# Down weights of a mixture-of-experts layer fetched with four consecutive rows per partition

## The chip, the cores and the metric

The kernel runs on one core of one Trainium2 chip, alone. The metric is the device time of one execution in microseconds, the median of the runs. Times from the trace are in microseconds (us) from the start of the span, or in nanoseconds (ns) where marked.

## The reference, cut to what matters

Two layers, each a mixer followed by a hierarchical mixture of experts (MoE) with 16 SwiGLU experts. There are 256 tokens of width 1024, the hidden width of an expert is 512, and every token goes to two experts. All arrays are float32.

```python
for e in range(N_EXPERTS):                                # 16
    hid = jax.nn.silu(xt @ w_gate[e]) * (xt @ w_up[e])    # (tokens, 1024) @ (1024, 512)
    y = y + gates[:, e:e + 1] * (hid @ w_down[e])         # (tokens, 512) @ (512, 1024)
```

The weights of one layer's experts are 96 MiB: 2 MiB each of gate, up and down per expert.

## The kernel before

**Stream of weights.** The host code builds one list, `order`, of pieces of 1 MiB, in the order in which they are consumed: for an expert two pieces of gate and two of up in turn (`gu`), and two of down (`dn`). `pump` issues them from the SP queue into 15 rotating buffers named `raw` (two more where space allows), each 128 partitions by 2048 float32, so a piece can be issued only when the piece that held its buffer has been used up. All of these issues are line 252. Experts that are not fixed beforehand (all but the first two) are known only when the router of that layer has run.

**Layout of the pieces.** Gate and up go in as `(p k) n -> p k n` with four of eight `k`: partition p gets four consecutive rows of 512 values, one run of 8 KiB. Down goes in as `(j p) n -> p j n` with two of four `j`: partition p gets rows 128 j + p of 1024 values, two separate runs of 4 KiB.

**Tasks.** Each expert's tokens are gathered into slots; the slots are cut into 20 tasks of 64 or 32 (8 of 64, 12 of 32), in the order `SEQ`. For a task, `gate_up` keeps the tokens stationary (`win`, or `hs` for expert 0) and streams the weights (`raw`). Since 64 or 32 tokens fill a half or a quarter of the array's columns, G = 2 or 4 matmuls on different column groups run at the same time, each with its own slice of the 512 hidden columns: 256 columns each at G = 2, 128 at G = 4. I call such a set of G matmuls a round. Every float32 matmul leaves two records, so a half task (4 k, gate and up) is 16 rounds in either form: 32 records at G = 2, 64 at G = 4. `hidden` takes Silu and the product, `turn` transposes 128 hidden columns at a time into `ht`, and `down` multiplies `ht` with the down weights, reading `raw` with a step of 8 values (32 bytes) because the 1024 outputs are kept as n k with k = 8. `project` moves the result out, and `combine` adds it up per token.

**Order.** SP and TensorE run in the order that is written out: first half of gate and up of task i+1, transposes of task i, second half of task i+1, down of task i. After task 9 (`LEFT`) every engine loads a count and passes a branch (`whatever_is_left`, lines 1433 and 1434; its body, `further`, runs only if tokens did not fit and is not entered here).

Of the kernel before, what the change touches and what calls it, by code (L numbers as in the profile page):

```python
# [19 lines left out]
P = 128  # L20
# [6 lines left out]
DE = 512  # L27
# [85 lines left out]
def trunk_kernel(ctx: ExitStack, tc: tile.TileContext, a, out, dbg=None):  # L113
    nc = tc.nc
    V, A, G, T = nc.vector, nc.scalar, nc.gpsimd, nc.tensor
# [9 lines left out]
    def bank(i):  # L125
        return pp.tile([P, 512], F32, name=f"b{i}", tag=f"b{i}")
# [4 lines left out]
    def k3(ap, k=KD):  # L131
        return ap.rearrange("p (k n) -> p k n", k=k)

    def mm(o, l, r, start=False, stop=False):
        T.matmul(o, l, r, start=start, stop=stop, skip_group_check=True)  # L135
# [30 lines left out]
    def moe(l):  # L166
        def at(name, p):
            if p < FIXED:
                return a[name][l, p]
            return lambda v: a[name][l, v]  # L170

        def gu(p):
            for h in range(2):
                for name in ("moe_w_gate", "moe_w_up"):
                    def cut(w, h=h):
                        return w.rearrange("(p k) n -> p k n", k=KD)[:, 4 * h:4 * h + 4, :]
                    order.append(("w", (name, l, p), (at(name, p), cut), 4))

        def dn(p):
            for h in range(2):  # L180
                def cut(w, h=h):
                    return w.rearrange("(j p) n -> p j n", p=P)[:, 2 * h:2 * h + 2, :]
                order.append(("w", ("moe_w_down", l, p), (at("moe_w_down", p), cut), 2))

        gu(0)
        for i, t in enumerate(TASKS):
            u = TASKS[i + 1] if i + 1 < len(TASKS) else None
            early = t["first"] and t["p"] < FIXED
            if early:
                dn(t["p"])  # L190
            if u and u["first"]:
                gu(u["p"])
            if t["first"] and not early:
                dn(t["p"])
# [265 lines left out]
    for i in range(4):  # L460
        b = bank(i)
# [841 lines left out]
    def place(rr, e, base, G):  # L1303

        pe = sb.tile([P, 2, P], BF, name="pe", tag="pt")
        for t in range(2):
            V.tensor_scalar(pe[:, t, :].rearrange("p (g w) -> p g w", g=G),
                            iota[:, 0:P // G].unsqueeze(1).to_broadcast([P, G, P // G]),
                            rr[:, t, e:e + 1], float(-base), op0=OP.subtract, op1=OP.is_equal)
        return pe  # L1310

    def moe_layer(l, before, then):
# [25 lines left out]
        def load_window(o, base, n, tag=None):  # L1338
            w = sb.tile([P, KD, n], F32, name="win", tag=tag or "sq", bufs=1 if tag else 3)
            A.copy(w, hs[:, :, ds(o + base, n) if base else ds(o, n)])  # L1340
            return w

        def slots(e, base, pe):
            b = bankbf(7)
            g = b[:, 512:518].bitcast(F32)
            for t in range(2):
                mm(g, pe[:, t, :], g3[:, t, e, :], start=(t == 0), stop=(t == 1))
            for t in range(2):
                T.transpose(b[:, t * P:(t + 1) * P], pe[:, t, :], identb)
            gs = sb.tile([P, 1], F32, name="gs", tag="gs1")  # L1350
            V.tensor_reduce(gs, g, AX.X, OP.add)
            ptt = sb.tile([P, S], F32R, name="ptt", tag="rs")
            A.copy(ptt, b[:, 0:S])
            return ptt, gs


        def gate_up(w, wts, b, G, halves=(0, 1)):
            n, r = DE // G, P // G
            for h in [x for f in halves for x in (2 * f, 2 * f + 1)]:
                i, src = h % 2, k3(wts[h], 4)  # L1360
                for kk in range(4):
                    for g in range(G):
                        mm(b[g * r:(g + 1) * r, i * n:(i + 1) * n], w[:, h // 2 * 4 + kk, :],
                           src[:, kk, g * n:(g + 1) * n], start=(h + kk == 0), stop=(h + kk == 6))

        def hidden(b, gs, G, tag="hid"):
            n = DE // G
            hid = sb.tile([P, n], F32, name="hid", tag=tag)
            A.activation(hid, b[:, 0:n], AF.Silu)  # L1369
            V.scalar_tensor_tensor(hid, hid, gs, b[:, n:2 * n], op0=OP.mult, op1=OP.mult)  # L1370
            return hid

        def turn(hid, b, G, tag="ht"):
            n, m = DE // G, DE // G // P
            for c in range(m):
                T.transpose(b[:, c * P:(c + 1) * P], hid[:, c * P:(c + 1) * P], ident)  # L1376
            ht = sb.tile([P, m, G, P // G], F32, name="ht", tag=tag)
            A.copy(ht.rearrange("p c g s -> p (c g s)"), b[:, 0:n])  # L1378
            return ht

        def down(ht, wts, G, bs2=(6,)):

            n, r, m, q = D // G, P // G, DE // G // P, KD // G
            ys = [bank(i) for i in bs2]
            y = [ys[g % len(ys)] for g in range(G)]
            for j in range(4):
                src = k3(wts[j // 2], 2)[:, j % 2, :].rearrange("p (n k) -> p n k", k=KD)
                for g in range(G):
                    mm(y[g][g * r:(g + 1) * r, 0:n], ht[:, j % m, j // m, :], src[:, :, q * g:q * (g + 1)],
                       start=(j == 0), stop=(j == 3))  # L1390
            return y
# [5 lines left out]
        def further(p, base, bk):  # L1397

            def load(name, tag, cut):
                r = sb.tile([P, 2048], F32, name="raw", tag=tag)  # L1400
                e = p if p < FIXED else nc.sync.value_load(exi[0:1, p:p + 1], min_val=0, max_val=NE - 1)
                nc.sync.dma_start(k3(r, 4 if name != "moe_w_down" else 2), cut(a[name][l, e]))
                return r

            tags = ("f8", "m8", "f8", "m8")
            wts = []
            for h in range(2):
                for name in ("moe_w_gate", "moe_w_up"):
                    wts.append(load(name, tags[len(wts)],
                                    lambda w: w.rearrange("(p k) n -> p k n", k=KD)[:, 4 * h:4 * h + 4, :]))  # L1410
                if h == 0:
                    b = bank(bk)
                    pt, gs = slots(p, base, place(rr, p, base, 2))
                    o = nc.scalar.value_load(ofi[0:1, 16 + p:17 + p], min_val=0, max_val=2 * S - base)
                    w = load_window(o, base, 64, "m8b")
                gate_up(w, wts, b, 2, (h,))
            ht = turn(hidden(b, gs, 2, "r8"), b, 2, "m8b")
            wts = [load("moe_w_down", tags[h], lambda w: w.rearrange("(j p) n -> p j n", p=P)[:, 2 * h:2 * h + 2, :])
                   for h in range(2)]
            y = down(ht, wts, 2)[0]  # L1420
            y2 = sb.tile([P, 2, 512], F32R, name="y2", tag="r8")
            A.copy(y2[:, 0, :], y)
            V.tensor_sub(y2[:, 1, :], y, y2[:, 0, :].bitcast(F32))
            for n in range(2):
                yx = y2[:, n, :]
                for kk in range(4):
                    for g in range(2):
                        k, rows = 4 * g + kk, slice(64 * g, 64 * g + 64)
                        mm(acc[k // 2][:, (k % 2) * S:(k % 2 + 1) * S],
                           yx.rearrange("p (n k) -> p k n", k=4)[rows, kk, :], pt[rows, :])  # L1430
# [10 lines left out]
        start, banks, wins, gates, packs, hid, gu, dw_ = {}, {}, {}, {}, {0: pe}, {}, {}, {}  # L1441
        n = len(TASKS)
# [30 lines left out]
        def first_half(i):  # L1473
            t = TASKS[i]
            p = t["p"]
            if t["first"]:
                gu[p] = take_all([(x, l, p) for x in ("moe_w_gate", "moe_w_up") * 2])
            banks[i] = bank(4 + i % 2)
            gate_up(wins[i], [w for w, _ in gu[p]], banks[i], P // t["n"], (0,))
            if t["last"]:  # L1480
                for _, x in gu[p][0:2]:
                    free(x)
# [48 lines left out]
        for i, t in enumerate(TASKS):  # L1531
# [11 lines left out]
            j = 0  # L1543
            if i + 2 < n:
                prepare(i + 2)
                if TASKS[i + 2]["pack"] > TASKS[i + 1]["pack"]:
                    j = TASKS[i + 2]["pack"]
# [25 lines left out]
    h = rms(drain_ada)  # L1573
# [21 lines left out]
    with in_order():  # L1595
# [23 lines left out]
        for t in range(2):  # L1619
            for i in range(4):  # L1620
                c = slice(2 * i, 2 * i + 2)
                src = k3(bk[i][:, t * S:(t + 1) * S], 2)
# [32 lines left out]
```

## Time and profile before

| | us |
|---|---|
| Runs before | 803.02, 805.72, 806.88 (median 805.72) |
| Profiled execution, its time | 803.79 |
| Profiled execution, its span | 802.0 |
| DMA data read from HBM | 285.69 MB |
| MoE of layer 0: stream of its routed pieces | about 185 to 406 |
| MoE of layer 1: stream of its routed pieces | about 564 to 783 |

[...] "A <- B" in a list of waits means that engine A stood idle until B was done.

### The profile page before, as it was taken

What the parts mean: (1) busy time and instruction counts of PE and PEld (TensorE: products, weight loads), DVE (VectorE), ACT (ScalarE), POOL (GpSimd) and SP (SyncE); (2) the same over time, 40 slices, a digit from 0 to 9 for tenths busy, and PEclk for the clock granted to TensorE, in tenths of its full rate; (3) what the DMA queues carried; (4) which work ended last, traced back from release to release, by engine and by line L of the source; (5) the groups of instructions that cost most, each with busy time, mean ns of one, the idle gap of its engine ahead of it and who ended that gap; (6) DMA issues with size and microseconds to landing.
All of it is one profiled execution on the core that took longest, in us unless ns stands there. A gap on an engine that the chain in (4) does not pass through costs nothing. (4 is left out here: it accounts for less than half of the span.)

```text
span 802.0 us, 18126 instructions
## 1 busy us (share of the span) xinstructions
PE 695.3 (87%) x7589; PEld 478.9 (60%) x7589; DVE 375.4 (47%) x866; ACT 236.8 (30%) x530; POOL 13.2 (2%) x33
## 2 busy tenths in 40 slices
PE   4699899978999959997669989998999995999765
PEld 3376358956666637544338878775666664755433
DVE  2516788877322212211158999997722231221114
ACT  3211143041222213211055326473322221321114
POOL 0010002000000000000000000000000000000000
PEclk9799899999999979999899999999999998999988
DMA  8989999967999999999999999321899999999991
GB/s 300 370 290 402 400 406 409 418 253 300 350 416 412 417 407 407 416 418 415 415 400 397 398 409 409 103 81 54 335 401 415 408 419 392 411 416 413 417 406 66
DMA packets 70029, 288.12 MB, mean 359 GB/s; under 512 B 8909, under 2 KB 11273, under 8 KB 53544
## 3 DMA queue, kind: packets, MB, share of 16 engines
q1 hardware_dynamic: 69928, 286.77, 90.1%
q8 instruction: 63, 1.03, 0.5%
q14 instruction: 38, 0.31, 0.1%
HBM read 285.69 MB, written 1.06 MB: 358 GB/s over the span
## 5 line engine op out<-in xcount | busy, mean ns | idle before, releaser
L135 PE MATMUL b<-raw,win 128*32 128x128 f32 (+1 forms) x3712 | 198.5, 309 | 36.3 <-DVEq L1434 16.9
L135 PEld LDWEIGHTS b<-raw,win 128*32 128x32 f32 (+1 forms) x3712 | 141.2, 120 | 85.7 <-issue 28.9
L1512 DVE TENSOR_TENSOR yp<-b,yp 32x256 fp32r<-32x256 f32 (+1 forms) x128 | 62.5, 488 | 143.5 <-ACT yp L1511 143.3
L135 PE MATMUL b<-raw,ht 128*32 128x256 f32 (+1 forms) x1024 | 113.5, 460 | 15.1 <-DMA raw<-in_moe_w_down_dram 15.0
L1511 ACT CAST yp<-b 32x256 fp32r<-32x256 f32 (+1 forms) x128 | 53.3, 417 | 131.0 <-PE b L135 93.2
L135 PEld LDWEIGHTS b<-raw,ht 128*32 128x32 f32 (+1 forms) x1024 | 42.1, 119 | 69.8 <-issue 34.5
L319 DVE SCALAR_TENSOR_TENSOR raw<-raw,csil 128x1024 f32<-128x1024 f32 x56 | 74.6, 1332 | 4.3 <-DMA raw<-in_w_ada_dram 3.2
L1370 DVE SCALAR_TENSOR_TENSOR hid<-hid,gs,b 128x128 f32<-128x128 f32 (+1 forms) x40 | 16.0, 401 | 113.4 <-ACT hid L1369 113.4
L914 DVE SCALAR_TENSOR_TENSOR ac<-hqk,dw,ac 128x256 f32<-128x256 f32 x120 | 50.7, 481 | 0.3
L135 PE MATMUL b<-h,raw 128*128 128x256 f32 x192 | 44.8, 392 | 5.3 <-ACT h L584 2.9
L135 PE MATMUL b<-hh,whf 128*128 128x256 f32 x160 | 41.7, 299 | 4.1 <-DVE whf L588 3.7
L135 PEld LDWEIGHTS b<-h,raw 128*128 128x128 f32 x192 | 37.1, 196 | 13.1 <-ACT h L584 3.8
L1369 ACT ACTIVATE hid<-b 128x128 f32<-128x128 f32 (+1 forms) x40 | 12.8, 320 | 105.5 <-PE b L135 105.5
L135 PE MATMUL b<-mx,raw 128*128 128x256 f32 x160 | 40.6, 409 | 0.0
L135 PEld LDWEIGHTS b<-mx,raw 128*128 128x128 f32 x160 | 38.8, 335 | 1.0 <-issue 0.8
L135 PE MATMUL b<-hl,whf 128*128 128x256 f32 x128 | 37.2, 290 | 0.4 <-DVE hl L849 0.4
L1378 ACT COPY ht<-b 128x128 f32<-128x128 f32 (+1 forms) x40 | 12.3, 308 | 84.6 <-PE b L1376 84.5
L1471 DVE TENSOR_REDUCE gs<-b 128x1 f32<-128x3 f32 x40 | 6.4, 161 | 65.9 <-PE b L135 65.5
L135 PE MATMUL b<-ptt,yp 128*128 128x256 f32 x224 | 34.4, 295 | 2.4 <-ACT yp L1511 1.6
L135 PEld LDWEIGHTS b<-hh,whf 128*128 128x128 f32 x160 | 29.7, 200 | 7.5 <-DVE whf L588 4.1
L135 PEld LDWEIGHTS b<-ptt,yp 128*128 128x128 f32 x224 | 28.4, 188 | 9.3 <-ACT yp L1511 6.6
L135 PE MATMUL b<-raw,h 128*128 128x512 f32 x64 | 31.5, 640 | 0.0
(287 smaller groups left out, 825.9 us busy)
## 6 DMA issues: line engine op xcount, KB each, us to landing
raw<-in_moe_w_gate_dram SPq DMA_DIRECT2D x64, 1024.0 KB, 13.1
raw<-in_moe_w_up_dram SPq DMA_DIRECT2D x64, 1024.0 KB, 14.7
raw<-in_moe_w_down_dram SPq DMA_DIRECT2D x64, 1024.0 KB, 16.5
raw<-in_w_ada_dram SPq DMA_DIRECT2D x48, 1024.0 KB, 15.8
raw<-in_ev_w_in_dram SPq DMA_DIRECT2D x10, 1024.0 KB, 13.1
raw<-in_od_w_in_dram SPq DMA_DIRECT2D x10, 1024.0 KB, 18.4
raw<-in_ev_w_out_dram SPq DMA_DIRECT2D x4, 1024.0 KB, 15.0
raw<-in_od_w_out_dram SPq DMA_DIRECT2D x4, 1024.0 KB, 14.0
```

Of the source, the lines that this page charges most:

```text
L135: T.matmul(o, l, r, start=start, stop=stop, skip_group_check=True)
L319: ins = V.scalar_tensor_tensor(acc, src, csil[:, k:k + 1], acc, op0=OP.mult, op1=OP.add)
L914: V.scalar_tensor_tensor(ac[:, m, :], src, dw[:, m, j:j + 1], ac[:, m, :], op0=OP.mult, op1=OP.add)
L1369: A.activation(hid, b[:, 0:n], AF.Silu)
L1370: V.scalar_tensor_tensor(hid, hid, gs, b[:, n:2 * n], op0=OP.mult, op1=OP.mult)
L1378: A.copy(ht.rearrange("p c g s -> p (c g s)"), b[:, 0:n])
L1471: V.tensor_reduce(gates[i], g, AX.X, OP.add)
L1511: A.copy(yh[o[0], o[1], :], src)
L1512: V.tensor_sub(yl[o[0], o[1], :], src, yh[o[0], o[1], :].bitcast(F32))
```

## The change

Down pieces are cut as `(p j) n -> p j n` with j = 4: partition p now gets rows 4 p + 2 h and 4 p + 2 h + 1 of half h, which lie next to each other in memory, one run of 8 KiB. Down's contraction for a given j is then over the hidden features 4 p + j, so the hidden columns have to come out in that order: `gate_up` streams the columns j, 4 + j, 8 + j, ... in place of a block of neighbours. Its moving operand is thus read with a step of four values (16 bytes). The output columns in PSUM are still contiguous. The number of matmuls, weight loads, DMAs and bytes is the same; `down`, `turn` and everything after them are untouched.

```diff
         def dn(p):
             for h in range(2):
                 def cut(w, h=h):
-                    return w.rearrange("(j p) n -> p j n", p=P)[:, 2 * h:2 * h + 2, :]
+                    return w.rearrange("(p j) n -> p j n", j=4)[:, 2 * h:2 * h + 2, :]
                 order.append(("w", ("moe_w_down", l, p), (at("moe_w_down", p), cut), 2))
...
         def gate_up(w, wts, b, G, halves=(0, 1)):
-            n, r = DE // G, P // G
+
+            n, r, m = DE // G, P // G, 4 // G
             for h in [x for f in halves for x in (2 * f, 2 * f + 1)]:
                 i, src = h % 2, k3(wts[h], 4)
                 for kk in range(4):
                     for g in range(G):
-                        mm(b[g * r:(g + 1) * r, i * n:(i + 1) * n], w[:, h // 2 * 4 + kk, :],
-                           src[:, kk, g * n:(g + 1) * n], start=(h + kk == 0), stop=(h + kk == 6))
+                        mm(k3(b[g * r:(g + 1) * r, i * n:(i + 1) * n], m), w[:, h // 2 * 4 + kk, :],
+                           src[:, kk, :].rearrange("q (p j) -> q j p", j=4)[:, m * g:m * g + m, :], start=(h + kk == 0), stop=(h + kk == 6))
```

The same cut is changed in `further`, which is not entered here.

## Rows read from the trace of the kernel before

**Rows 1.** The page: the DMA packets of the whole span, counted by size.

```profile
DMA packets 70029, 288.12 MB, mean 359 GB/s; under 512 B 8909, under 2 KB 11273, under 8 KB 53544
```

**Rows 2.** Windows, by stage: stretch, length, busy us of each engine, clock, DMA.

```profile
185.00:290.00 105.00, 102.40 (x1594) 67.53 (x1594) 34.35 (x109) 28.41 (x73) 0.00 (x0) 0.99 0.99 398
290.00:410.00 120.00, 94.68 (x1294) 57.94 (x1295) 23.10 (x57) 25.69 (x64) 0.20 (x1) 0.93 1.02 412
...
500.00:563.00 63.00, 56.80 (x418) 45.05 (x418) 55.24 (x147) 33.23 (x70) 1.03 (x2) 0.99 0.24 84
563.00:665.00 102.00, 101.41 (x1585) 67.02 (x1585) 35.02 (x113) 28.49 (x72) 0.00 (x0) 0.99 0.99 402
```

**Rows 3.** Waits of the SP queue, 185 to 283: us in total, times, longest.

```profile
SPq L252 <- PE b L135: 65.0, 30, 9.2
```

**Rows 4.** Waits of the SP queue, 699 to 757.

```profile
SPq L252 <- DMA raw<-in_moe_w_gate_dram: 15.2, 8, 2.0
...
SPq L252 <- PE b L135: 0.7, 2, 0.4
```

**Rows 5.** Timeline of SP, 699 to 765: start, us, engine, line, issue.

```profile
699.45 0.35 SPq L252 DMA_DIRECT2D raw<-in_moe_w_gate_dram  x1
...
729.56 0.34 SPq L252 DMA_DIRECT2D raw<-in_moe_w_gate_dram  x1
...
734.85 0.33 SPq L252 DMA_DIRECT2D raw<-in_moe_w_gate_dram  x1
737.35 0.33 SPq L252 DMA_DIRECT2D raw<-in_moe_w_up_dram  x1
739.83 2.88 SPq L252 DMA_DIRECT2D raw<-in_moe_w_down_dram  x2
```

**Rows 6.** DMA issues in 185 to 406, then in 563 to 785.

```profile
raw<-in_moe_w_down_dram SPq DMA_DIRECT2D x28, 1024.0 KB, 18.2
...
raw<-in_moe_w_down_dram SPq DMA_DIRECT2D x28, 1024.0 KB, 17.2
```

**Rows 7.** Timeline of PE, 236 to 262: gate and up, then down, each form.

```profile
238.36 1.92 PE L135 MATMUL b<-raw,win 128*32 128x128 f32 x64
240.11 2.01 PE L135 MATMUL b<-raw,ht 128*32 128x256 f32 x32
...
246.69 3.65 PE L135 MATMUL b<-raw,win 128*64 128x256 f32 x32
...
258.87 3.65 PE L135 MATMUL b<-raw,ht 128*64 128x512 f32 x16
```

**Rows 8.** Groups by line, forms kept apart: two kinds of weight loads in the mixers.

```profile
L135 PEld LDWEIGHTS b<-mx,raw 128*128 128x128 f32 x160 | 38.8, 335 | 1.0 <-issue 0.8 <-ACT m8b L730 0.2
L135 PEld LDWEIGHTS b<-h,raw 128*128 128x128 f32 x192 | 37.1, 196 | 13.1 <-ACT h L584 3.8 <-DMA raw<-in_ev_w_in_dram 3.6 <-issue 0.6
```

**Rows 9.** Windows at the start of layer 0's experts.

```profile
200.00:210.00 10.00, 10.00 (x174) 5.64 (x174) 0.99 (x3) 1.03 (x3) 0.00 (x0) 1.00 0.93 361
210.00:220.00 10.00, 10.00 (x211) 6.95 (x211) 5.25 (x15) 4.70 (x12) 0.00 (x0) 1.00 0.90 336
```

**Rows 10.** Timeline of SP around the branches of both layers.

```profile
284.85 0.34 SPq L252 DMA_DIRECT2D raw<-in_moe_w_up_dram  x1
...
299.11 0.39 SPq L252 DMA_DIRECT2D raw<-in_moe_w_down_dram  x1
...
663.14 0.33 SPq L252 DMA_DIRECT2D raw<-in_moe_w_up_dram  x1
...
676.90 2.02 SPq L252 DMA_DIRECT2D raw<-in_moe_w_down_dram  x2
```

**Rows 11.** Line 252: landing of the single issues at 284.85, 663.14 and 518.4.

```profile
DMA to landing us min/median/max: 18.7/18.7/18.7
...
DMA to landing us min/median/max: 17.9/17.9/17.9
...
DMA to landing us min/median/max: 5.0/5.0/5.0
```

More of the change, by code (lines that the diff above doesn't have):

```diff
@@ L1417, in further @@
             ht = turn(hidden(b, gs, 2, "r8"), b, 2, "m8b")
-            wts = [load("moe_w_down", tags[h], lambda w: w.rearrange("(j p) n -> p j n", p=P)[:, 2 * h:2 * h + 2, :])
+            wts = [load("moe_w_down", tags[h], lambda w: w.rearrange("(p j) n -> p j n", j=4)[:, 2 * h:2 * h + 2, :])
                    for h in range(2)]
```

## The prediction

> **What bounds the kernel now.** I read the windows by stage first, then who holds up the SP queue, then the spacing of its issues. In both MoE stretches the DMA engines are busy nearly without a break (0.99 up to the branch at about 400 GB/s, 1.02 behind it at 412), and TensorE is just as busy in the first half of each, 102.4 of 105 us and 101.4 of 102 us [rows 2]. So two things run close together, and the reader should see which one gives way when. From 185 to 283 SP waits 65.0 us for TensorE to give buffers back [rows 3]: pieces are issued when TensorE allows it, and only the pieces already in flight keep the DMA engines fed. From 699 to 757 SP waits for landings and hardly for TensorE, 0.7 us [rows 4]: here the DMA stream is the bound, up to the last four down pieces and the short tail behind them. Between the layers the mixer has TensorE and VectorE busy at about nine tenths [rows 2]; it starts when the experts of layer 0 end, and around 500 to 563 the DMA share falls to 0.24 because layer 1's experts aren't known yet. So what layer 0 saves moves the mixer forward, what layer 1 saves moves the end forward, and down pieces that land before their router has run are worth nothing. That leaves 28 down pieces in each layer [rows 6].
>
> **The gain.** In the stretch where issues follow landings, their spacing is the time of one piece. Gate and up: 734.85, 737.35, 739.83, so 2.50 and 2.48, 2.49 on average [rows 5]. From 699.45 to 729.56 lie two experts, eight gate or up and four down pieces, in 30.11 us [rows 5]. The down pieces have 30.11 - 8 x 2.49 = 10.19, or 2.55 each. Down costs 0.06 us more per MiB. The packets say why: 70,029 - 53,544 = 16,485 are of 8 KiB or more [rows 1], which is 128 for each of the 128 gate and up pieces, while down comes in 256 packets of 4 KiB. Afterwards a down piece has the shape that a gate piece has today (128 runs of 8 KiB, one every 16 KiB of memory), so I take its price, 2.49. Gain: 28 x 0.06 = 1.7 us per layer, 3.4 us in both; the nearest other reading, 0.055 to 0.065, gives 3.1 to 3.6. It cannot be more unless something else than the down pieces gets faster. SP's own issue time is not on this path.
>
> [...]
>
> **The price on TensorE.** `gate_up` now streams its moving operand with a step of 16 bytes. No row shows this step, but `down` already streams with a step of 32, in both forms [rows 7]. All rows are at full clock:
> - Two column groups, contiguous: 32 records, 16 rounds, 3.65 us for 16 x 256 columns. With the step: 16 records, 8 rounds, 3.65 us for 8 x 512 columns. The same number of columns in the same time: the step costs nothing.
> - Four column groups, contiguous: 64 records, 16 rounds in 1.92 us. The last record stands about 0.27 us and the four start within 0.02, so a round takes (1.92 - 0.29) / 15 = 109 ns for 128 columns. With the step: 32 records, 8 rounds in 2.01 us, the last about 0.39; (2.01 - 0.41) / 7 = 229 ns for 256 columns, or 114.5 for 128. The step costs 5.5 ns a round, 5%.
>
> I take these prices: nothing for tasks of 64, 32 rounds x 5.5 ns = 0.18 us for each of the 12 tasks of 32 per layer. Below, the bound is zero (a step of 16 bytes touches memory more densely than one of 32). Above, it is the largest price of a step in this trace: a contiguous weight load stands 196 ns, one whose operand is read with a step of 32 bytes 335 ns [rows 8], a factor of 1.7. I choose the low value because [rows 7] is the same operand of the same engine in the same array form.
>
> **Where this price is hidden and where not.** In the DMA-bound second half TensorE waits for landings anyway; there it is free, and so is the tail, since the last four pieces are down pieces whose matmuls don't change. In the first half TensorE paces the issues. Two places matter.
>
> The start of layer 0: the DMA share is 0.93 and 0.90 from 200 to 220 [rows 9], the engines run dry because SP waits for buffers. Two tasks of 32 lie before that, 0.4 us lost directly. I charge none to the start of layer 1, whose stretch up to the branch moves 402 GB/s against 398 [rows 2].
>
> The branch after task 9: SP issues nothing from 284.85 to 299.11 and from 663.14 to 676.90 [rows 10]. The pieces in flight bridge it: the last one lands 18.7 and 17.9 us after its issue, at 303.5 and 681.0, and a piece issued into an empty queue needs 5.0 us [rows 11], 2.5 more than the spacing. To keep pace the next issue had to come at 301.0 and 678.5; it came 1.9 and 1.6 us earlier. That is all the slack there is. It shrinks twice. The stream itself is earlier by its own gain, some 12 down pieces x 0.06 = 0.7 us, which leaves 1.2 and 0.9. And TensorE is later: of the tasks streamed up to the branch seven are of 32, the last of them half done, 6.5 x 0.18 = 1.2 us. In layer 0, 0.4 of that has already been lost to the stream as well, so nothing is left to lose; in layer 1 about 0.3 us. After the branch TensorE has idle time and the lateness ends.
>
> Sum: -3.4 + 0.4 + 0.3 = **-2.7 us**. Against the profiled execution's own 803.79 (span 802.0 and 1.8 around it) that is 801.1. But this execution lies 1.9 below the median of the runs, 805.72; the four executions shown average 804.85, which I take as the level of before, and so forecast **802.2**. In the sum, "a piece in flight is enough" is the cover everything rests on: with D the lateness of TensorE at the branch, each microsecond of D beyond about 1 in each layer is paid in full, twice.
>
> **Rivals.**
> 1. *The step costs nothing at all in the new order.* Then D = 0 and the whole 3.4 us stays: 801.4. For it: the step is half of the one in `down`, and the form with two groups shows none. Against: the form with four does.
> 2. *Neighbouring streams collide, and the kernel gets slower.* In `down` with two groups, the two streams read addresses 16 bytes apart; with four groups they are 8 apart, two in each 16 bytes, and only there a price shows. After the change all streams of a round read within the same 16 bytes, two or four of them. If each further stream in the same 16 bytes costs the same 5% of a round, the form with two pays 11 ns and the form with four three times 5.5. D at the branch is then 6.5 x 32 x 16.5 ns + 4 tasks of 64 x 32 x 11 ns = 3.4 + 1.4 = 4.8 us. Loss 4.8 - 1.2 + 4.8 - 0.9 = 7.5, less the gain of 3.4: +4.1 us, 809.0. It decides the sign once D is above 2.8 us, about 8 ns on every round. Against: nothing but two points supports the rule of addition.
> 3. *A step past 16 bytes is slow in itself*, as the weight loads in [rows 8] suggest. At their factor of 1.7 a round of 109 ns becomes 185 and one of 218 becomes 371; 12 x 32 x 76 ns + 8 x 32 x 153 ns = 68 us more per layer, while TensorE idles about 3 us ahead of the branch and 25 behind it [rows 2], so some 40 us per layer are left over: about 885. Against: both stepped forms in [rows 7]. [...]
> 4. *The packet size isn't why down is slower*, and the pieces stay at 2.55. Then only the price at the start remains, +0.4: 805.2. For it: only the packets' length is seen to differ, not that it acts. Against: the two kinds of pieces otherwise move the same bytes by the same queue.
>
> **How the numbers follow.** Forecast 0.45, rival 1 0.25, rival 2 0.15, rival 3 0.04, rival 4 0.11. A measurement of this kernel can tell about 0.5%, 4.0 us, from no change. The forecast, rival 1 and rival 4 all lie within it, but rival 1 and the forecast's better end (3.1 to 3.6) are close to the edge, and runs of before scatter by 3.9 us; I give a quarter of their chance to faster. Faster 0.19, same 0.63, slower 0.18. The range goes from the lowest run of before with the largest gain, 803.02 - 3.6 = 799.4, to just short of rival 2's time, 808.5, because runs scatter and a smaller collision is likelier than a full one.
>
> **What would show it.** Right: packets of 8 KiB or more rise by some 8,190 and the total falls as much; issues that follow landings are 2.49 apart for all kinds; an expert takes 14.94 us in place of 15.06; rounds of `gate_up` at four groups take 109 to 115 ns and at two 216 to 218; the stretch from the first routed issue to the last landing in layer 1 is about 1.4 us shorter. Wrong: longer groups of 32 records at two groups (over 3.7 us); more or deeper drops of the DMA share at 200 to 220 and behind the branches; a down piece that still takes 2.55.

## The result, and the profile after

| | us |
|---|---|
| Before, median of the runs beside the change | 806.04 |
| After, median | 955.96 (952.89 to 959.32) |
| Ratio | 1.1873, 95% interval 1.1829 to 1.1917 |
| Span of the traced executions, before and after | 802.0 and 951.5 |

The kernel became 150 us slower, where 2.7 us less had been forecast and 808.5 was the upper end of the range. Of the two things that the change does, one came about as worked out, the gain on the DMA stream. The other, the price on TensorE, was wrong by a factor of more than 20: 5.5 ns a round had been put down for tasks of 32, and 120 ns came.

The page of the changed kernel: busy time and share of TensorE, the packets by size, and the engines and lines of the chain that ended last.

```profile
PE 884.1 (93%) x7589; PEld 510.4 (54%) x7589; DVE 375.4 (39%) x866; ACT 237.3 (25%) x530; POOL 13.2 (1%) x33
...
DMA packets 61837, 288.12 MB, mean 303 GB/s; under 512 B 8909, under 2 KB 11273, under 8 KB 37160
...
PE b L135 14%; PE b L1377 0%; ACT yp L1512 0%; DVE ot L1625 0%; DVE yp L1513 0%; ACT L331 0%; DVE xT L1564 0%; PE bh L1458 0%; ACT sq L1059 0%; PE b L1607 0%; DVEq L1652 0%; ACT vt L1070 0%; ACT rt L1618 0%; ACT ht L1379 0%; ACT rt L1619 0%
```

The packets are what they should be: 61,837 - 37,160 = 24,677 of 8 KiB or more, 8,192 more than in [rows 1], and 8,192 fewer in all. So the down pieces do come in runs of 8 KiB. But no DMA is left in the chain that ended last. The timeline of PE, for the same four forms as [rows 7], says why.

```profile
236.09 7.46 PE L135 MATMUL b<-raw,win 128*64 128x256 f32 x32
243.48 2.05 PE L135 MATMUL b<-raw,ht 128*32 128x256 f32 x32
...
255.29 3.65 PE L135 MATMUL b<-raw,ht 128*64 128x512 f32 x16
258.88 3.85 PE L135 MATMUL b<-raw,win 128*32 128x128 f32 x64
```

The two `down` rows are what they were, 2.05 for 2.01 and 3.65 for 3.65. The two `gate_up` rows, which the change gave a step of 16 bytes, went from 1.92 to 3.85 and from 3.65 to 7.46. From here on I give the time of a round from the records themselves: the median, over all groups of one form, of the time from the start of a record to the start of the one G places later. That is 109 ns before and 229 after at four groups, 216 and 451 at two, a factor of 2.1 in both.

The waits of the SP queue, from 185 to 330 (answers to [rows 3]) and from 850 to 903 (answers to [rows 4]):

```profile
SPq L252 <- PE b L135: 111.5, 30, 17.7
SPq L252 <- PE b L1377: 6.4, 3, 3.3
```

```profile
SPq L252 <- PE b L135: 33.4, 12, 5.0
SPq L252 <- PE b L1377: 6.8, 2, 3.4
SPq L252 <- PE bh L1458: 1.3, 1, 1.3
```

In the late stretch, where SP had waited for landings, it now waits for TensorE alone. Right behind the branch SP still waits 4.7 us for landings (337 to 449), but TensorE waits for no landing anywhere in the experts: the DMA stream is no longer what bounds them. The windows of the changed kernel, cut at its branches, show the same (columns as in [rows 2]: the length, then busy us and records of PE, PEld, DVE, ACT and POOL, then the granted clock with full speed as 1.00, the DMA share, that is how busy the DMA engines were on average, and GB/s):

```profile
181.00:337.00 156.00, 154.50 (x1583) 76.09 (x1584) 34.52 (x109) 27.64 (x71) 0.00 (x0) 1.00 0.74 283
337.00:449.00 112.00, 106.18 (x906) 47.06 (x904) 15.27 (x39) 17.41 (x45) 0.20 (x1) 0.98 0.95 386
...
636.00:791.00 155.00, 154.74 (x1576) 76.23 (x1576) 34.17 (x107) 27.54 (x71) 0.00 (x0) 0.99 0.74 283
```

TensorE is busy without a break up to each branch while the DMA share falls from 0.99 [rows 2] to 0.74. The clock is not the cause, it is at 0.99 to 1.00 there.

**Where the 150 us are.** Each round costs 120 ns more at four groups and 235 at two, so a task of 32 costs 32 x 0.120 = 3.84 us more and a task of 64 costs 7.52. The last issue ahead of the branch of layer 1, at 663.14 before and 790.93 now, follows the end of the second half of task 10. PE around that half, before and now, with the matmuls of `combine` (b<-ptt,yp) just ahead of it:

```profile
658.15 2.79 PE L135 MATMUL b<-ptt,yp 128*128 128x256 f32 x16
...
661.15 1.92 PE L135 MATMUL b<-raw,win 128*32 128x128 f32 x64
```

```profile
784.66 2.16 PE L135 MATMUL b<-ptt,yp 128*128 128x256 f32 x16
...
787.03 3.85 PE L135 MATMUL b<-raw,win 128*32 128x128 f32 x64
```

So seven tasks of 32 and four of 64 are streamed by then, 26.9 + 30.1 = 57.0 us more. In the trace, that issue came 99.3 us after the first routed one (563.87 to 663.14), and now comes 154.6 after it (636.35 to 790.93): 55.3 more. The difference lies between the halves: a `combine` stands between the halves of a task three times ahead of the branch, and each time the second half now starts 0.6 us sooner after the first.

Behind the branch five tasks of 32 and four of 64 are streamed, 49.3 us more, but from there to the end it is only 160.6 in place of 138.9 us, 21.7 more. The windows from that last issue to the end, before and now:

```profile
663.14:802.00 138.86, 105.77 (x1356) 63.82 (x1355) 29.75 (x73) 32.91 (x77) 0.00 (x0) 0.92 0.89 360
```

```profile
790.93:951.52 160.59, 145.06 (x1356) 69.00 (x1356) 29.74 (x73) 32.98 (x77) 0.00 (x0) 0.98 0.72 288
```

TensorE's idle time fell by 17.6 us, from 33.1 to 15.5. Its busy time grew by 39.3 and not by 49.3. A part of these 10 us is the clock: before, more of the work there ran at the lower level (0.92 on average, 0.98 now), and a round of contiguous columns that takes 109 ns at full clock takes 213 there, while the stepped round takes 229 to 230 at both levels. The rest of the 10 us was not taken apart. Layer 0 gives 54.6 and 21.0 in the same way. With the 3.1 us by which this execution reached its experts earlier, the four add up to 149.5, the difference of the spans.

### The profile page after: what moved, and what is told of

Same layout as the page of the kernel before. It is cut to its first block, busy times and chain, and to the rows that moved or that the text cites. A ratio compares the mean times of both kernels' runs of the same rounds, so it can differ in the third digit from the quotient of the medians.

```text
span 951.5 us, 18126 instructions
## 1 busy us (share of the span) xinstructions
PE 884.1 (93%) x7589; PEld 510.4 (54%) x7589; DVE 375.4 (39%) x866; ACT 237.3 (25%) x530; POOL 13.2 (1%) x33
## 2 busy tenths in 40 slices
DMA packets 61837, 288.12 MB, mean 303 GB/s; under 512 B 8909, under 2 KB 11273, under 8 KB 37160
## 5 line engine op out<-in xcount | busy, mean ns | idle before, releaser
L135 PE MATMUL b<-raw,win 128*32 128x128 f32 (+1 forms) x3712 | 378.0, 462 | 11.7 <-DVEq L1435 11.7
L135 PEld LDWEIGHTS b<-raw,win 128*32 128x32 f32 (+1 forms) x3712 | 169.1, 133 | 188.8 <-issue 136.5
L135 PE MATMUL b<-raw,ht 128*32 128x256 f32 (+1 forms) x1024 | 107.4, 445 | 1.0 <-ACT ht L1379 1.0
L135 PE MATMUL b<-raw,hs 128*32 128x128 f32 (+1 forms) x384 | 45.2, 483 | 0.0
L135 PE MATMUL b<-ptt,yp 128*128 128x256 f32 x224 | 32.0, 296 | 4.3 <-ACT yp L1512 4.3
```

## The experiments

Four theories stood against each other once the rounds were seen. *Line*: what counts is how many values a stream takes in turn from each aligned 16 bytes of SBUF, a line from here on; one costs the factor of 2.1, two cost what `down` pays before, 5% at four groups. *Collision*: the streams of one round disturb each other because they read in the same line. *Any step*: any operand that isn't contiguous is slow. *Layout*: the new down pieces have a part in the loss. In e1, e2, e8, e9 and e12 the weights that meet don't belong together, so they measure time only.

**e1, the down pieces alone.** `gate_up` as before.

```diff
-                    return w.rearrange("(j p) n -> p j n", p=P)[:, 2 * h:2 * h + 2, :]
+                    return w.rearrange("(p j) n -> p j n", j=4)[:, 2 * h:2 * h + 2, :]
```

> Only the down pieces change: four consecutive rows per partition, gate_up as before with contiguous columns. (The hidden columns then don't meet the rows of down that belong to them; nothing of the work is left out.) If the price of a down piece falls from 2.55 to 2.49 us as worked out before: 56 routed pieces x 0.06 = 3.4 us less, ratio 0.9958, packets of 8 KiB or more up by 8,192, an expert's six pieces 14.94 us apart where issues follow landings. If the length of the packets isn't why down is slower: no change, ratio 0.9995 to 1.0005, six pieces still 15.06 us apart.

Measured: 802.74 against 805.92, ratio 0.9952 (0.9926 to 0.9979). The timeline of SP where issues follow landings, to be held against [rows 5], and below it the pair of down pieces before:

```profile
713.38 0.33 SPq L252 DMA_DIRECT2D raw<-in_moe_w_gate_dram  x1
...
723.38 2.82 SPq L252 DMA_DIRECT2D raw<-in_moe_w_down_dram  x2
728.35 0.33 SPq L252 DMA_DIRECT2D raw<-in_moe_w_gate_dram  x1
...
743.28 0.33 SPq L252 DMA_DIRECT2D raw<-in_moe_w_gate_dram  x1
```

```profile
709.43 2.89 SPq L252 DMA_DIRECT2D raw<-in_moe_w_down_dram  x2
714.50 0.35 SPq L252 DMA_DIRECT2D raw<-in_moe_w_gate_dram  x1
```

Two experts lie between the gate issues, 29.90 us where [rows 5] has 30.11; 29.88 was worked out. The pair of down pieces by itself took 5.07 us before and takes 4.97 here, 0.05 us less for each piece, which would make 2.8 us in all in place of 3.4. This half of the prediction holds: down pieces now cost what gate pieces cost, and the time is 0.48% less; the runs can't tell 2.8 us (0.35%) from 3.4 (0.42%).

**e2, the step alone.** The down pieces as before, `gate_up` as in the change.

> Only gate_up changes: its moving operand read with a step of 16 bytes, the down pieces as before (so hidden columns and rows of down don't belong together). If the whole loss is TensorE's: rounds at four groups 229 ns and at two 451 ns as in the changed kernel, time 954 to 960 us, since almost nowhere the stream of pieces is the bound any more. If the new down pieces had a part in the loss (an access pattern that is bad for memory or for the matmuls of down): clearly under 950 us.

Measured: 956.48 us, rounds 229 and 451 ns. The whole loss is the step's; *layout* is out.

**e3, a step of two.** The same runs of 8 KiB, with pairs of rows in place of fours:

```diff
-                    return w.rearrange("(p j) n -> p j n", j=4)[:, 2 * h:2 * h + 2, :]
+                    return w.rearrange("(h p j) n -> h p j n", h=2, j=2)[h]
...
-                           src[:, kk, :].rearrange("q (p j) -> q j p", j=4)[:, m * g:m * g + m, :], start=(h + kk == 0), stop=(h + kk == 6))
+                           src[:, kk, 2 * P * (m * g // 2):2 * P * (m * g // 2 + 1)].rearrange("q (p j) -> q j p", j=2)[:, m * g % 2:m * g % 2 + m, :], start=(h + kk == 0), stop=(h + kk == 6))
```

> Pairs instead of fours: half h of down gives partition p the rows 256 h + 2 p and 256 h + 2 p + 1 (one run of 8 KiB, as in the change), gate_up reads with a step of two values (8 bytes). Theory 'line': what counts is how many values a stream takes in turn from one 16-byte line; one costs double, two cost what down pays today (two neighbours of eight: 5% at four groups). Then rounds at four groups 109 to 115 ns, at two 216 to 228, and the time is 802 to 804 us against 806.0. Theory 'collision' (streams of one round in the same line): two streams of a round share lines at four groups, none at two, so 216 at two groups and between 115 and 229 at four; at half the loss, 170 ns, 12 x 32 x 60 ns = 23 us per layer of which some 13 stay, about 830 us. Theory 'any step': as in the changed kernel, about 956 us.

Its rows of PE:

```profile
241.91 2.04 PE L135 MATMUL b<-raw,win 128*32 128x128 f32 x64
...
245.95 4.06 PE L135 MATMUL b<-raw,win 128*64 128x256 f32 x32
```

Rounds of 115 and 227 ns: a step is not slow in itself, *any step* is out. At two groups even streams that share no line pay 5%. The time, 809.63, ratio 1.0024 (0.9989 to 1.0058), missed the 802 to 804 that were expected; more on that below.

**e4, the streams apart.** The changed kernel, but group g takes the four k in rotated order, which leaves the sum the same and puts the streams of a round 2 KiB apart.

```diff
+                        q = (kk + g) % 4
-                        mm(k3(b[g * r:(g + 1) * r, i * n:(i + 1) * n], m), w[:, h // 2 * 4 + kk, :],
-                           src[:, kk, :].rearrange("q (p j) -> q j p", j=4)[:, m * g:m * g + m, :], start=(h + kk == 0), stop=(h + kk == 6))
+                        mm(k3(b[g * r:(g + 1) * r, i * n:(i + 1) * n], m), w[:, h // 2 * 4 + q, :],
+                           src[:, q, :].rearrange("q (p j) -> q j p", j=4)[:, m * g:m * g + m, :], start=(h + kk == 0), stop=(h + kk == 6))
```

> The changed kernel, but group g takes the four k of a half in rotated order, k = (kk + g) mod 4, so that the streams of a round are 2 KiB apart in each partition and never in the same 16-byte line. Theory 'collision': the rounds fall back to 109 to 115 ns and 216 to 228, time 802 to 806 us. Theory 'line': each stream by itself takes one value per line, so nothing changes: 229 and 451 ns, 953 to 959 us.

```profile
225.94 3.92 PE L135 MATMUL b<-raw,win 128*32 128x128 f32 x64
231.86 7.42 PE L135 MATMUL b<-raw,win 128*64 128x256 f32 x32
```

Measured: 958.33 us, rounds 229 and 451 as in the change. *Collision* is out: each stream pays for itself.

**e8 and e9, other patterns.** Only the moving operand of `gate_up` differs from before. e8: at two groups pairs of neighbours, one pair every 16 bytes; at four groups single values every 32 bytes. e9: at two groups pairs every 32 bytes that start at the last value of a line; at four groups single values every 12 bytes.

```diff
 # e8
+                        if G == 2:
+                            s = src[:, kk, :].rearrange("q (p j) -> q p j", j=4)[:, :, 2 * g:2 * g + 2]
+                        else:
+                            s = wts[h][:, kk // 2 * 1024:(kk // 2 + 1) * 1024].rearrange("q (p j) -> q j p", j=8)[:, kk % 2 * 4 + g, :]
 # e9
+                        if G == 2:
+                            c = kk // 2 * 1016
+                            s = wts[h][:, c + 8 * g:c + 8 * g + 1024].rearrange("q (p j) -> q p j", j=8)[:, :, 3:5]
+                        else:
+                            s = src[:, kk, 0:384].rearrange("q (p j) -> q j p", j=3)[:, g % 3, :]
```

> gate_up with two other access patterns, the down pieces as before; which weights meet which tokens is then no longer right. Tasks of 64: runs of two neighbours, one run every 16 bytes (as down reads at four groups, every 32). Tasks of 32: single values with a step of eight (32 bytes). Theory 'line': two values per line 216 to 227 ns a round at two groups, one value per line 229 ns at four, whatever the step. If the step counts and not the line: the rounds at four groups longer than 229 ns, and those at two groups longer than the 227 ns of e3.

> gate_up with two more access patterns, down as before; the weights that meet the tokens are not the right ones, some are read twice and some not at all, the work is as long. Tasks of 64: pairs of neighbours, one pair every 32 bytes as in down, but starting at the fourth value of a 16-byte line, so the two lie in two lines. Tasks of 32: single values with a step of three (12 bytes), so of four values two share a line. Theory 'line': the pairs cost as much as single values, 451 ns a round at two groups; the step of three lies between, about (2 x 0.87 + 2 x 1.79) / 4 ns a value, 170 ns a round at four groups. Theory 'run length' (two neighbours in memory are enough, wherever they lie): pairs 216 to 227 ns, step of three 229 ns like any step without neighbours.

Rows of PE in e8, then in e9:

```profile
230.90 3.82 PE L135 MATMUL b<-raw,win 128*64 128x256 f32 x32
...
242.75 3.90 PE L135 MATMUL b<-raw,win 128*32 128x128 f32 x64
```

```profile
236.06 7.41 PE L135 MATMUL b<-raw,win 128*64 128x256 f32 x32
...
245.27 2.99 PE L135 MATMUL b<-raw,win 128*32 128x128 f32 x64
```

e8: 227 ns at two groups, 233 at four, 857.91 us in its one execution. The step hardly matters, 32 bytes cost within 2% what 16 cost. e9 (one execution, 919.14 us): the pairs across a line boundary cost 452 ns, like single values, although they are as much neighbours as those of `down`; and the step of three costs 173 ns, where *line* had 170. That is the case that tells the line from the length of the run. The size of the line follows as well: a unit of 8 bytes would have made the step of two in e3 slow (one value from each), and a unit of 32 would have made the step of four fast (two from each). *Line* gave the time of every round in e3, e4, e8 and e9 in advance, to within 4 ns.

**e5 and e10, a mixture.** Row pairs as in e3; tasks of 64 stream contiguous columns, and Silu and the product read the bank with a step of two to put them in order; tasks of 32 stream with a step of two.

```diff
+                        s = src[:, kk, g * n:(g + 1) * n]
+                        if G == 4:
+                            s = src[:, kk, g // 2 * 2 * P:(g // 2 + 1) * 2 * P].rearrange("q (p j) -> q j p", j=2)[:, g % 2, :]
...
+            gate, up, o = b[:, 0:n], b[:, n:2 * n], hid
+            if G == 2:
+                gate, up = [x.rearrange("q (p j) -> q j p", j=2) for x in (gate, up)]
+                o = k3(hid, 2)
```

> Down as in e3 (row pairs, runs of 8 KiB). Tasks of 64 stream contiguous columns again and put them in order where Silu and the product read the bank (a step of two values there); only tasks of 32 stream with a step of two. Rounds at two groups then 216 ns, at four 115 ns. If the lateness at the branch is all that spoils e3: D = 6.5 x 32 x 5.5 ns = 1.2 us as in the forecast, and the time is 2.7 us below before, ratio 0.9967. If e3's loss was something else than its rounds (the row pairs in memory): 1.000 to 1.003 again. If the stepped reads of Silu and product cost: hid longer than 320 ns on ScalarE and 401 ns on VectorE.

Measured: 805.28 against 805.24, ratio 1.0004 (0.9985 to 1.0024); rounds 216 and 115 ns; what the stepped reads of Silu and the product took is not shown. The gain that was expected isn't there. I repeated it beside the kernel before and e1's kernel, on one chip.

> e5 once more, for its trace and beside e11 and e12 on one chip. If the gain was lost to the lateness of TensorE at the branch: the stretch from the first routed issue to the last one in a layer is no shorter than before (200.9 and 198.7 us). If it is kept there and lost behind it, to the clock that TensorE was granted at the end of each layer's experts (0.57 where before had 0.92 in the traced executions): that stretch is shorter by 1 us or more, and the time changes with the clock from execution to execution.

> The kernel before, run as if it were a changed one: ratio 1.000, and its interval tells what a difference of a few tenths of a per cent is worth here. Its trace shows whether the granted clock at the end of the experts and the length of the last 40 us repeat (0.92 in the traced execution) or change from execution to execution.

> e1 once more, beside e10 and e11: ratio 0.995 to 0.997 if its gain is that of the shorter pieces (3.4 us), 1.000 if e1 was luck. If it holds here too while e10 stays at 1.000, the 5.5 ns a round at four groups are worth the whole gain.

Ratios: e10 1.0000 (0.9974 to 1.0025), e11 1.0002 (0.9970 to 1.0033), e12 0.9974 (0.9942 to 1.0006). One suspicion was the clock granted about and behind the last landing. Ten microseconds there (stretch, length, busy time and records of PE, granted clock, DMA), first the kernel before in its first trace, then e10, then e11:

```profile
782.50:792.50 10.00, 8.62 (x68) 0.92 0.04 14
```

```profile
780.00:790.00 10.00, 9.15 (x52) 0.57 0.03 11
```

```profile
778.00:788.00 10.00, 9.00 (x55) 0.59 0.02 7
```

In e11 the kernel before has the low clock there too, 0.59 where its first trace had 0.92; so the clock is not what sets e5 apart. From the first routed issue to that of the last down piece, both layers together take 399.6 and 399.9 us before, 398.2 and 398.0 in e1 and e12, 398.2 and 398.8 in e5 and e10. That is too close to say where e5 loses what e1 keeps; it stays open, and with e10 and e12 the intervals overlap. None of the versions in which hidden columns and rows of down belong together beat the kernel before.

**e6 and e7, the change for some experts alone.** `if p >= 8` and `if p >= 14` in front of both cuts; the other experts as before.

> The change for experts 8 to 15 alone, which have only tasks of 32 (the other experts as before, down and gate_up both). A half task of 16 rounds takes 16 x 120 ns longer, a task 3.84 us. Theory 'slack': three such tasks (11.5 us) lie before the branch, where only some 1.7 us are covered, so about 9.8 us are lost per layer; the five behind it (19.2 us) disappear in the 25 us of TensorE's idle time there. With 32 down pieces at 0.06 us less: 2 x 9.8 - 1.9 = 17.7 us more, about 823.6. Theory 'every round counts': 8 x 3.84 x 2 = 61 us more, 867. Theory 'all hidden in the share of idle time': no change.

> The change for experts 14 and 15 alone, the last two tasks of each layer, where issues follow landings. Theory 'slack': 2 x 3.84 us more of TensorE in each layer are hidden behind landings, apart from the last half task of a layer, whose 16 rounds (1.9 us more) run while the last four down pieces land: no change, or 0.5 us less, 805 to 806. Theory 'every round counts': 4 x 3.84 = 15.4 us more, 821.

e7: ratio 0.9998 (0.9970 to 1.0027). Rounds more than twice as long cost nothing where landings are the bound. e6: 828.07 against 805.24, ratio 1.0274 (1.0231 to 1.0317), so 22.1 us more (18.6 to 25.5) where *slack* had 17.7 and *every round counts* 61. SP around the branch of layer 0:

```profile
297.20 0.34 SPq L254 DMA_DIRECT2D raw<-in_moe_w_up_dram  x1
...
311.19 0.34 SPq L254 DMA_DIRECT2D raw<-in_moe_w_down_dram  x1
```

The last issue ahead of it comes 110.7 us after the first routed one (186.46), in place of 100.3: the three tasks of 32 before it are there almost in full, 10.5 of 11.5 us, and 10.9 in layer 1. Behind the branch 19.2 us more of TensorE in each layer lengthen the way only by 1.4 and 2.8 us. So the split at the branch is right, and the cover that I had counted at it, some 1.7 us, isn't seen.

## Why the prediction was wrong, point by point

- **What bounds the kernel**: right. TensorE paces the issues up to the branch, landings pace them behind it; a price on TensorE is paid in the one (e6, 10.5 of 11.5 us) and not in the other (e7, ratio 0.9998).
- **The gain**: right in what makes it, and in size as far as the runs can tell: 0.05 to 0.06 us for a down piece, 2.8 to 3.4 us in all (e1 0.48% less, e12 0.26%; the intervals hold both, but that of e12 holds zero too). The stated 3.1 to 3.6 was too narrow: the pair of down pieces, 5.07 and 4.97 us, gives 2.8.
- **The price on TensorE is the step that failed.** It said that `down` "already streams with a step of 32, in both forms", and took its rounds as the price of a step. The text ahead of the prediction says it in the same way, and both are wrong. `down` reads `src[:, :, q * g:q * (g + 1)]` of a view p n k: the neighbours k are the inner dimension, q = 2 of them at four groups and q = 4 at two, and only the n lie 32 bytes apart. It takes two or four values from each line. The rows give only the whole size of the operand (128x256, 128x512), so [rows 7] fit both readings, and the code, which was there, was not read to the inner dimension. The 5% at four groups was the price of two values per line; a moving operand with a single value per line had no row at all. With the prices measured (120 and 235 ns a round) the same sum, 6.5 tasks of 32 and 4 of 64, gives D = 55.1 us in place of 1.2. The count has a slip too: the seventh task of 32 is done at the last issue and not half done, which at the price forecast is 0.09 us and at the measured one 1.9.
- **The bound from above** was there: the weight loads of [rows 8] that read with a step pay a factor of 1.7. The text set it aside as farther than [rows 7]; it was nearer, as that operand does take one value per line. It should have kept its end in the range and a good part of the chance.
- **Rival 3 is what happened**, with a factor of 2.1 in place of 1.7; only, what is slow is one value from each line and not a long step (e8's pairs cost 5%, and so do those of `down`, 32 bytes apart). Its own sum at 2.1 is 12 x 3.84 + 8 x 7.52 = 106 us per layer, less 28 of idle time, 78 twice: 156 us on 804.85, or 961, and 956 was measured. It had a chance of 0.04 because the same misreading spoke against it. The kernel before and after, e3 and e8 put numbers to it: 0.84 to 0.85 ns a value with four values from each line, 0.89 to 0.90 with two, 1.76 to 1.82 with one.
- **Rival 2**, the collision, is refuted by e4. **Rival 4**, that packets don't matter, by e1 and its spacing.
- **The slack at the branch**, 1.9 and 1.6 us: not found. If none is counted, and seven tasks of 32 are counted, the sums are -3.4 + 2 x 2.6 = +1.8 for e3, -3.4 + 2 x 1.2 = -1.0 for e5 and 2 x 11.5 - 1.9 = 21.1 for e6, against +1.9, +0.3 and +22.1 measured, all within their intervals. That was worked out afterwards and not tried by itself; a queue that looks 1.9 us deep on one landing is not a reserve to build a sum on.

## What to carry to other kernels

Before a row is used as the price of an access pattern, read the innermost dimension of the operand in the code: the size that a row shows is the same for one value every 32 bytes and for four neighbours every 32 bytes, and the time may not be. A layout that makes a transfer's runs longer by interleaving rows moves the interleave to whoever reads the other operand; here 0.05 to 0.06 us per piece were bought with 120 to 235 ns on every round. Where an engine and the DMA stream take turns as the bound, price each half by itself, and prefer to pay where the stream is late anyway (e7).

## What the runs showed of the hardware

- A moving operand in float32 at full clock, time per value of one stream: 0.84 to 0.85 ns contiguous (216 and 109 ns a round before), 0.89 to 0.90 with two values from each 16-byte line (227 and 115 in e3 with steps of two, 227 in e8 with pairs within a line), 1.35 with a step of three (173 in e9), 1.76 to 1.82 with one (451 and 229 in the change, 233 in e8). Each is a round divided by its 128 or 256 columns.
- Worked out afterwards, these rows fit one sum, an estimate from the rounds above: 1.79 ns for each line that a stream opens (229 / 128), or the time of contiguous values where that is longer. Pairs come to 1.79 / 2 = 0.90 ns a value, a step of three, which opens three lines for four values, to 1.34, and single values to 1.79.
- The clock is a test of it that the traces hold already. At the lower level, 0.50, a round at four groups takes 213 ns (1.66 a value) with contiguous values before, and the 256 columns of `down`, pairs, take 427 (213 for 128); in the change a round with single values takes 230 ns, where it takes 229 at full clock. So the time of single values did not follow the clock, and what doubled a round at full clock adds 8% to one at half. A half task of 32 before, contiguous, at 0.50, then one of the changed kernel at 0.69 (at full clock 1.92 and 3.85 us; stretch, length, busy time and records of PE, granted clock, DMA):

```profile
297.01:300.65 3.64, 3.64 (x64) 0.50 0.98 386
```

```profile
345.67:349.56 3.89, 3.89 (x64) 0.69 0.18 40
```

- It counts per stream: the factor is the same with two and with four streams (451 / 216 and 229 / 109, both 2.1), and doesn't depend on whether they share lines (e4, 229 and 451 again). What counts is the line and not the neighbourhood: pairs across a line boundary cost 1.77 ns a value (e9, 452 ns a round).
- Weight loads show the same direction: 335 ns with a step of 32 bytes, 196 contiguous [rows 8].
- Where issues follow landings, a 1 MiB piece in runs of 8 KiB takes 2.48 to 2.50 us, one in runs of 4 KiB 2.53 to 2.55 ([rows 5], the kernel before, e1).
- The granted clock about and behind the last landing differed from one traced execution of the same kernel to the next, 0.92 and 0.59 for the kernel before (e11).
